# Where the first weight load of the later output projections stands in the program

## The chip, the cores and the metric

The kernel runs on one core of one Trainium2 chip. The metric is the time of one launch on the device in microseconds (us); lower is better. One execution was also taken by the profiler. A core has a matrix engine (TensorE, PE in the profile, with its weight loads as PEld), three engines for elementwise work (VectorE or DVE, ScalarE or ACT, GpSimd or POOL) and SyncE (SP), which here issues nearly all transfers between HBM and the on-chip memory (SBUF). Matmuls write to PSUM, the accumulation memory.

## The reference

One layer of a hybrid encoder is computed for 2048 new prompt frames and 32 frames of a running stream ("sample rows"), with width 1024. All is float32:

```python
h = rms_norm(x, g_norm1) * (1 + scale1) + shift1          # scales from c @ w_ada
q, k, v, z, xbc_raw, dt_raw = jnp.split(h @ w_in, SPLITS, axis=-1)
...
attn = stick_breaking(q, k, v)                            # 8 heads of 64, gated by a running product
attn = rms_norm(attn.reshape(bsz, l, SB_WIDTH), g_attn_out)
ssm, new_conv, new_ssm = ssd_mixer(z, xbc_raw, dt_raw, ...)   # conv, chunked scan, gate, rms_norm
mixed = jnp.concatenate([attn, ssm], axis=-1) @ w_out     # the output projection
x = x + gate1 * mixed
h2 = rms_norm(x, g_norm2) * (1 + scale2) + shift2
ff = (jax.nn.silu(h2 @ w_gate) * (h2 @ w_up)) @ w_down    # 2816 hidden columns
x = x + gate2 * ff
```

Returned are the new x for both inputs, and the keys, values, convolution rows and scan states.

## The kernel before, in words

**Arithmetic.** A float32 product is made of three matmuls on rounded operands: each operand is split into a high part (a copy in the reduced format, ScalarE) and a low part (the rest, by a subtraction on another engine). `mm3` (L127) issues high x high, high x low and low x high.

**Tiling and stages.** The prompt is cut into four quarters of 512 frames, g = 0 to 3; the sample rows count as g = 4. The first stage makes h, the input projection and the scan mixer, quarter by quarter. Attention follows: quarter 0 in full (`attn`), quarters 1 to 3 in a window of the last 640 keys (`attn_w`, L341), and then `far_keys` (L453), one pass over the older keys for the few rows that still need them. It walks seven chunks of 256 keys (tiles `Kf`, `Vf`), adds what it finds to the stored attention rows (`far`, `aof`), and closes. Then come the output projections (class `Wout`, L717) and the feed-forward (`ffn`, L885).

**The output projection of a quarter.** `Wout.pre` (L728) loads the scan mixer's rows (`mH`, `mL`, high and low) from the scratch tensor `mixT`, the gates (`gr`) and the rows of x (`x`, summed in place). It also holds `pf`, a list of four pieces of `w_out`, two column halves for the scan rows and two for the attention rows; I call them out A, B, C and D. `opiece` (L103) makes a piece: one load of 1024 KB into a `wr` buffer, then four times a ScalarE activation (L114) that scales by the group's norm weight and rounds into `wh`, and a VectorE operation (L115) for the low part `wl`. `Pieces.get` (L97) hands out a piece and at once asks for the next (`fill`, L93). `product` (L748) multiplies a half for four blocks of 128 frames into PSUM (tile `z`), scales by the gate into `tm` (L761) and adds to x on GpSimd (L763). `ssm` (L767) does out A and B. `rows` (L774) loads and splits the attention rows, and `run` (L838) does C and D and then the second norm, whose result goes to the scratch tensor `h2D`. `project` (L995) strings these together for one quarter.

**The feed-forward of a quarter** walks eleven pieces of 256 hidden columns. Each has a gate, an up and a down piece of weights, 1024 KB each, made by the same loads into `wr` and splits into `wh` and `wl` (ScalarE and GpSimd, L59 and L60). A piece has 96 matmuls for gate and up (tiles `pg`, `pu`) and 48 for down (`py`). Again each `get` asks for the next piece, so the up and the down weights of a piece are asked for at its start, and the next gate weights ahead of its down products.

**Shared buffers.** All weight pieces, of output projection and feed-forward alike, come from `wtiles` (L72): two `wr` buffers, three `wh` and three `wl`.

**What sets the order.** From `attn_w` of quarter 1 on, two generators are woven together by `merge` (L1700). Side A is `streamA` (L1619): the windows of quarters 1 to 3, the far keys, the projections of quarters 1 and 2, the sample rows' attention and projection, and the projection of quarter 3. Side F is `streamF`, the feed-forward of the four quarters. Each `yield` carries a planned cost in ns. A step of A with cost c adds c times a ratio to a debt, and F is stepped until the debt is paid. The ratio begins at a constant (L1642) and becomes 4.0 when quarter 1 is projected (L1631). F must not begin quarter g + 1 before A has said that it is projected (`("need", g + 1)`, L966).

The text so made is a program order. The framework (`schedule_with_timeline_sim`, L1752) then puts each instruction into its engine's queue where, in a plan of the run that it makes while building, the operands and a free buffer are there; where several are ready, the earlier one in the program goes first. So a load that needs nothing but a buffer can stand in SyncE's queue far ahead of its neighbours in the code.

The pool of a projection's own tiles (`gr`, `x1` and others) is opened for each quarter (L1626) on the memory that the attention's tiles held before.

Of the kernel before, what the change touches and what calls it, by code (L numbers as in the profile page):

```python
# [35 lines left out]
def body(tc, nc, I, O):  # L36
    V, A, G, PE = nc.vector, nc.scalar, nc.gpsimd, nc.tensor
    ctx = ExitStack()
    with ctx:
# [12 lines left out]
        def load(dst, src):  # L52
            nc.sync.dma_start(dst, src)
# [49 lines left out]
        def opiece(k0, hf, g, pool=None):  # L103

            if pool is None:
                r, h, l = wtiles()
            else:
                r = rpool[0].tile([P, WP], F32, tag="wr", name="wr", bufs=rpool[1])
                h, l = (pool.tile([P, 2048], F32R, tag=t, name=t, bufs=1) for t in ("oh", "ol"))
            v = lambda t: t[:, :2048].rearrange("p (k c) -> p k c", k=4)  # L110
            load(v(r), I["w_out"][0, k0 * P:(k0 + 4) * P, hf * 512:(hf + 1) * 512].rearrange("(k p) c -> p k c", p=P))
            r, h, l = v(r), v(h), v(l)
            for k in range(4):
                A.activation(h[:, k, :], r[:, k, :], AF.Copy, scale=g[:, k:k + 1])  # L114
                V.scalar_tensor_tensor(l[:, k, :], r[:, k, :], g[:, k:k + 1], h[:, k, :].bitcast(F32), op0=ALU.mult, op1=ALU.subtract)  # L115
            return h, l
# [81 lines left out]
        def mixed(mp):  # L198

            return [mp.tile([P, 4, 512], F32R, name=t) for t in ("mH", "mL")], mp.tile([P, 4, 4], F32, name="stat")  # L200
# [227 lines left out]
        def window_tiles(at_):  # L428
            aT = [at_.tile([P, 2, 257], F32, tag="aT", name=f"aT{i}", bufs=2) for i in range(2)]
            dd = at_.tile([P, 2, 257], mybir.dt.bfloat16, tag="d1", name="dd", bufs=1)  # L430
            for t in aT + [dd]:
                G.memset(t, 0.0)
            G.memset(dd[:, :, 256:257], 1.0)
            return aT, dd
# [3 lines left out]
        def far_consts(fc):  # L438
            io = fc.tile([P, 256], mybir.dt.bfloat16, name="io")
            G.iota(io, pattern=[[1, 256]], base=0, channel_multiplier=0, allow_small_or_imprecise_dtypes=True)  # L440
            pcol = fc.tile([P, 1], F32, name="pcol")
            G.iota(pcol, pattern=[[0, 1]], base=0, channel_multiplier=1, allow_small_or_imprecise_dtypes=True)
            hv = fc.tile([P, 9], F32, name="hv")
            G.iota(hv, pattern=[[16, 9]], base=1, channel_multiplier=0, allow_small_or_imprecise_dtypes=True)
            vt = fc.tile([P, NH, 12], F32, name="vt")
            G.iota(vt, pattern=[[16, NH], [1, 12]], base=5, channel_multiplier=0, allow_small_or_imprecise_dtypes=True)
            bk = fc.tile([P, 4], F32, name="bk")
            G.iota(bk, pattern=[[P, 4]], base=0, channel_multiplier=0, allow_small_or_imprecise_dtypes=True)
            one = fc.tile([P, P], F32R, name="one")
            G.memset(one.bitcast(F32), 1.0)  # L450
            far_c.update(io=io, pcol=pcol, hv=hv, vt=vt, bk=bk, one=one, pool=fc)
# [265 lines left out]
        class Wout:  # L717
# [10 lines left out]
            def pre(self):  # L728

                s, t0 = self.s, self.t0  # L730
                mH, mL = mHL
                for i, t in enumerate((mH, mL if s == 0 else mH[:, :, DEC:])):
                    load(t[:, :, :self.n].bitcast(F32), mixT[i, :, :, t0:t0 + self.n].rearrange("k p t -> p k t"))
                self.pf = Pieces([lambda k=k, hf=hf, g=g: opiece(k, hf, g) for k, g in ((4, gsc), (0, gac)) for hf in range(2)])
                self.pf.fill(1)
                xsrc = I["x_prompt"][0, t0:t0 + self.n] if s == 0 else I["x_sample"][0]
                self.gr, self.x1 = [], {}
                for hf in range(2):
                    t = self.tile("gr", "gr")
                    load(t.rearrange("p (m c) -> p m c", m=4), modD[16 + hf * 4:20 + hf * 4, s].unsqueeze(0).to_broadcast([P, 4, P]))  # L740
                    self.gr.append(t)
                for b, c, m in self.tb:
                    x1 = self.tile("x1", "x1", nb=len(self.tb), w=D)
                    load(x1[:m], xsrc[c:c + m])
                    for hf in range(2):
                        self.x1[hf, b] = x1[:, hf * 512:(hf + 1) * 512]
# [248 lines left out]
        def project(g, pool):  # L995
            w = Wout(g, pool, zps)
            w.pre()
            yield 3000
            yield from w.ssm()
            yield from w.run()  # L1000

# [40 lines left out]
        with ExitStack() as pa:  # L1042
# [454 lines left out]
            def run_all(g):  # L1497
                for _ in g:
                    pass
# [40 lines left out]
            def chain(*gs):  # L1540
                for g in gs:
                    yield from g
# [56 lines left out]
        with ExitStack() as pb_:  # L1599
            mp = pb_.enter_context(tc.tile_pool(name="mp", bufs=1))  # L1600
            mHL, stat = mixed(mp)
            pw0 = ExitStack()
            w0 = Wout(0, pw0.enter_context(tc.tile_pool(name="wo0", bufs=1)), dense_ps)
            w0.pre()
            merge2(a0, w0.ssm(), R1)
            pa0.close()
            fc = px_.enter_context(tc.tile_pool(name="fc", bufs=1, side="right"))
            far_consts(fc)
            L = fc.tile([P, NH, 12], F32, name="L")
            px1 = ExitStack()  # L1610
            at1 = px1.enter_context(tc.tile_pool(name="at1", bufs=1, side="right"))
            wt = window_tiles(at1)
            a1 = chain(*(attn_w(g, at1, L, wt) for g in range(1, NQ)))
            run_all(w0.run())
            pw0.close()
            fp = pb_.enter_context(tc.tile_pool(name="fp", bufs=1))
            late = {}

            def streamA():  # L1619
                yield from a1  # L1620
                yield from far_keys(at1, wt[0], L)
                px1.close()
                for g in range(1, NQ):
                    if g == 3:
                        yield from part_s()
                    with tc.tile_pool(name=f"wo{g}", bufs=1, side="right") as wo:  # L1626
                        yield from project(g, wo)
                    if g < 3:
                        yield ("done", g)
                    if g == 1:  # L1630
                        yield ("ratio", 4.0)  # L1631
                px_.close()
                late["ex"] = pb_.enter_context(tc.tile_pool(name="ex", bufs=1, side="right"))
                dpool[0] = pb_.enter_context(tc.tile_pool(name="pdF", bufs=5, space=PSUM))
                yield ("done", 3)

            def streamF():
                hT = load_h(0, fp, None)
                for g in range(NQ):
                    hT = yield from ffn(g, fp, late, hT)  # L1640

            merge(streamA(), streamF(), 1.55)  # L1642


        fx = ctx.enter_context(tc.tile_pool(name="fx", bufs=1))
# [39 lines left out]
def merge2(main, side, ratio, fin=True):  # L1685

    debt = 0.0
    for c in main:
        debt += c * ratio
        while side is not None and debt > 0:  # L1690
            try:
                debt -= max(next(side), 1)
            except StopIteration:
                side = None
    if side is not None and fin:
        for _ in side:
            pass


def merge(a, f, ratio):  # L1700
    done, debt = set(), 0.0
    a_live, f_live, need = True, True, None
    while a_live or f_live:
        blocked = a_live and need is not None and need not in done
        if not blocked:
            need = None
        if a_live and (blocked or not f_live or debt <= 0):
            try:
                c = next(a)
                if isinstance(c, tuple) and c[0] == "ratio":  # L1710
                    ratio = c[1]
                elif isinstance(c, tuple):
                    done.add(c[1])
                elif not blocked:
                    debt += c * ratio
            except StopIteration:
                a_live = False
        else:
            try:
                c = next(f)  # L1720
                if isinstance(c, tuple):
                    need = c[1]
                else:
                    debt -= c
            except StopIteration:
                f_live = False
# [29 lines left out]
```

## Time and profile before

| | |
|---|---|
| time, median of 3 runs (lowest, highest) | 2942.09 us (2938.08, 2947.04) |
| time of the profiled execution | 2940.34 us |
| its span, first to last instruction | 2938.4 us |
| mean granted clock of TensorE, as a share of full speed | 0.963 |
| busy: PE, PEld | 2729.8 us (93%), 2334.2 us (79%) |
| busy: DVE, ACT, POOL | 1563.9, 1186.0, 1532.6 us |
| moved by DMA | 466.54 MB, mean 159 GB/s |

How to read the lines. A row of a timeline has the start in us from the span's start, the length in us, the engine (SPq is SyncE's queue, where a row is the issue of a transfer), the line of the code (of a helper where a helper issues it), the operation, output tile <- input tiles, the shape, and the count of merged instructions. In square brackets stands how long the engine had been idle before and what released it. A row of a table of stretches has the stretch, its length, then busy us and count of instructions for each engine, then the granted clock of TensorE, the busy share of the DMA engines and GB/s. Matmuls overlap in such counts: a row of 0.39 us is followed by the next start after 0.23.

### The profile page before, as it was taken

Reading aid. Unit: us, or ns where it says so; the run is one execution under the profiler, and the core shown is the slowest. Engines: PE = TensorE matmul, PEld = TensorE weight load, DVE = VectorE, ACT = ScalarE, POOL = GpSimd, SP = SyncE. Lnnn points to the kernel's source line nnn. Section 1 sums busy time; section 2 is a strip of 40 time slices with the busy share of each in tenths; the row PEclk is TensorE's granted clock in tenths of the full one; section 3 lists DMA queues with packets and bytes.
Section 4 is the critical chain, followed back from the end, with each engine's and each line's share of the span. In section 5 each row is a group of like instructions: output and inputs, shape, how many; then the busy total and the mean of one; then the engine's idle time right before and its main releaser. Section 6 shows DMA issues by size and latency. Waiting matters only on the chain.

```text
span 2938.4 us, 41844 instructions
## 1 busy us (share of the span) xinstructions
PE 2729.8 (93%) x15467; PEld 2334.2 (79%) x15467; DVE 1563.9 (53%) x2575; ACT 1186.0 (40%) x2533; POOL 1532.6 (52%) x1318
## 2 busy tenths in 40 slices
PE   6998998998978689998879999999999999999998
PEld 5988997896977578876667887777787788899997
DVE  6577586766568567874344534434434422333336
ACT  6466365555535455522224334333243422322221
POOL 4767566564654635743136655544564445544445
PEclk8999998999988789999989999999999999999999
DMA  8755653463467787837745744534733722422221
GB/s 266 219 171 153 202 177 114 119 182 106 131 175 237 193 225 196 208 116 213 199 165 180 258 135 137 152 122 155 236 127 106 230 88 92 154 87 87 86 87 66
DMA packets 415619, 466.54 MB, mean 159 GB/s; under 512 B 34191, under 2 KB 330991, under 8 KB 415406
## 3 DMA queue, kind: packets, MB, share of 16 engines
q1 hardware_dynamic: 414478, 463.61, 52.7%
q8 instruction: 124, 2.03, 0.3%
q14 instruction: 89, 0.73, 0.1%
q10 hardware_dynamic: 896, 0.14, 0.0%
q0 software_dynamic: 32, 0.03, 0.0%
HBM read 372.66 MB, written 91.04 MB: 158 GB/s over the span
## 4 chain that ended last, share of the span: by engine, by line
PE 57%; DVE 6%; DMA 5%; issue 3%; POOL 2%; ACT 2%; SPq 1%; DVEq 0%; ACTq 0%; POOLq 0%
PE pg L130 5%; PE pg L131 5%; PE pg L132 5%; PE pu L130 5%; PE pu L131 5%; PE pu L132 5%; PE py L130 5%; PE py L131 4%; PE py L132 4%; PE z L130 2%; PE z L131 2%; PE z L132 1%; PE d L131 1%; PE d L130 1%; PE d L132 1%
## 5 line engine op out<-in xcount | busy, mean ns | idle before, releaser
L60 POOL TENSOR_TENSOR wl<-wr,wh 128x512 fp32r<-128x512 f32 x752 | 1010.3, 1375 | 861.7 <-ACT wh L59 778.5
L59 ACT ACTIVATE wh<-wr 128x512 fp32r<-128x512 f32 x816 | 450.3, 620 | 512.3 <-PE py L132 128.4
L130 PE MATMUL d<-wh,hH 128*128 128x256 f32 (+2 forms) x1088 | 316.0, 291 | 18.8 <-ACT hH L59 10.9
L132 PE MATMUL d<-wh,hL 128*128 128x256 f32 (+2 forms) x1088 | 311.8, 287 | 6.7 <-POOL hL L60 6.7
L130 PE MATMUL pg<-h,wh 128*128 128x512 f32 (+1 forms) x880 | 311.3, 354 | 3.7 <-POOL aT L378 2.5
L130 PE MATMUL pu<-h,wh 128*128 128x512 f32 (+1 forms) x880 | 310.5, 353 | 1.2 <-DVE sg L952 1.2
L131 PE MATMUL d<-wl,hH 128*128 128x256 f32 (+2 forms) x1088 | 311.4, 286 | 0.0
L132 PE MATMUL pg<-h,wl 128*128 128x512 f32 (+1 forms) x880 | 310.7, 353 | 0.6 <-POOL wl L60 0.6
L131 PE MATMUL pg<-h,wh 128*128 128x512 f32 (+1 forms) x880 | 310.7, 353 | 0.0
L132 PE MATMUL pu<-h,wl 128*128 128x512 f32 (+1 forms) x880 | 310.5, 353 | 0.0
L131 PE MATMUL pu<-h,wh 128*128 128x512 f32 (+1 forms) x880 | 309.9, 352 | 0.0
L130 PE MATMUL py<-wh,aH 128*128 128x512 f32 x704 | 282.5, 401 | 7.0 <-DVE ya L983 5.0
L131 PE MATMUL py<-wl,aH 128*128 128x512 f32 x704 | 277.0, 394 | 0.0
L983 DVE TENSOR_TENSOR ya<-py,ya 128x512 f32<-128x512 f32 x288 | 190.4, 684 | 148.4 <-PE py L132 146.8
L132 PE MATMUL py<-wh,aL 128*128 128x512 f32 x704 | 265.8, 394 | 2.8 <-DVE aL L60 2.8
L952 DVE TENSOR_TENSOR sg<-pg,sg 128x512 f32<-128x512 f32 (+1 forms) x110 | 64.8, 589 | 336.8 <-ACT sg L951 336.8
L130 PEld LDWEIGHTS d<-wh,hH 128*128 128x128 f32 (+1 forms) x1088 | 207.7, 191 | 23.2 <-ACT hH L59 12.5
L132 PEld LDWEIGHTS d<-wh,hL 128*128 128x128 f32 (+1 forms) x1088 | 206.9, 190 | 8.0 <-POOL hL L60 7.2
L131 PEld LDWEIGHTS d<-wl,hH 128*128 128x128 f32 (+1 forms) x1088 | 207.3, 191 | 0.7
L130 PEld LDWEIGHTS pg<-h,wh 128*128 128x128 f32 x880 | 165.6, 188 | 28.5 <-POOL aT L378 2.7
L130 PEld LDWEIGHTS pu<-h,wh 128*128 128x128 f32 x880 | 165.5, 188 | 24.2 <-DVE sg L952 1.4
L132 PEld LDWEIGHTS pg<-h,wl 128*128 128x128 f32 x880 | 165.4, 188 | 24.1 <-POOL wl L60 1.1
(434 smaller groups left out, 5686.7 us busy)
## 6 DMA issues: line engine op xcount, KB each, us to landing
wr<-in_w_in SPq DMA_DIRECT2D x48, 1024.0 KB
wr<-in_w_gate SPq DMA_DIRECT2D x44, 1024.0 KB
wr<-in_w_up SPq DMA_DIRECT2D x44, 1024.0 KB
wr<-in_w_down SPq DMA_DIRECT2D x44, 1024.0 KB
wr<-in_w_ada SPq DMA_DIRECT2D x24, 1024.0 KB
wr<-in_w_out SPq DMA_DIRECT2D x20, 1024.0 KB
h2D<-hl SPq DMA_DIRECT2D x64, 256.0 KB
Kw<-KT SPq DMA_DIRECT2D x48, 320.0 KB
```

The lines of the kernel that those rows point to most:

```text
L59: A.activation(h, src, AF.Copy)
L60: (eng or V).tensor_tensor(l, src, h.bitcast(F32), op=ALU.subtract)
L130: PE.matmul(out, lhsT=sh, rhs=mh, start=(i == 0), stop=False)
L131: PE.matmul(out, lhsT=sh, rhs=ml, start=False, stop=False)
L132: PE.matmul(out, lhsT=sl, rhs=mh, start=False, stop=(i == n - 1))
L952: V.tensor_tensor(sg[:, :n], pg[:, :n], sg[:, :n], op=ALU.mult)
L983: V.tensor_tensor(dst, ps[:r], dst, op=ALU.add)
```

## The change

```diff
@@ Wout.pre @@
                 self.pf = Pieces([lambda k=k, hf=hf, g=g: opiece(k, hf, g) for k, g in ((4, gsc), (0, gac)) for hf in range(2)])
-                self.pf.fill(1)
+                if self.g == 0:
+                    self.pf.fill(1)
                 xsrc = I["x_prompt"][0, t0:t0 + self.n] if s == 0 else I["x_sample"][0]
@@ project @@
             w.pre()
-            yield 3000
+            yield 3500
+            w.pf.fill(1)
+            yield 4500
             yield from w.ssm()
@@ body @@
-            merge(streamA(), streamF(), 1.55)
+            merge(streamA(), streamF(), 1.45)
```

Before, `pre` asks for out A between the loads of the scan rows and those of gates and x, and `project` then gives the other side 3000 times the ratio. After, only quarter 0, whose projection isn't woven by `merge`, still does so. For quarters 1 to 3 and the sample rows, `project` gives way for 3500, asks for out A (load, four activations, four VectorE operations), gives way for 4500, and goes on to the products, which ask for out B. The ratio of the weaving until quarter 1 is projected falls from 1.55 to 1.45. No arithmetic changes.

## The prediction

> **What bounds the kernel now.** I read the page first, then busy time by stretches, then the timelines of SyncE, ScalarE and TensorE around each output projection.
>
> ```profile
> span 2938.4 us, 41844 instructions
> ...
> PE 57%; DVE 6%; DMA 5%; issue 3%; POOL 2%; ACT 2%; SPq 1%; DVEq 0%; ACTq 0%; POOLq 0%
> ```
>
> The chain that ended last is mostly TensorE (PE). So an edit that moves no arithmetic can change the time only where PE stands idle or runs at its lower clock. The stretches show where that is (columns: length, then busy time and count of PE, PEld, DVE, ACT, POOL, then the granted clock and the DMA share):
>
> ```profile
> 1265.00:1430.00 165.00, 149.84 (x704) 119.93 (x703) 80.13 (x146) 41.62 (x81) 52.26 (x40) 1.00 0.63 176
> 1430.00:1502.00 72.00, 49.99 (x165) 36.11 (x166) 27.58 (x49) 4.47 (x10) 7.74 (x6) 0.74 0.67 214
> 1502.00:2340.00 838.00, 826.52 (x3653) 661.46 (x3652) 356.09 (x518) 310.66 (x622) 445.17 (x355) 1.00 0.51 163
> ```
>
> From 1502 to 2340, which holds the projections of quarters 2, the sample rows and 3, PE is idle for 838.0 - 826.5 = 11.5 us in all; there is little to win there. One matmul costs 826.52 / 3653 = 0.226 us there, the price I use below. The bad place is 1430 to 1502, the end of the far keys and the start of quarter 1's projection: 22.0 us idle and a mean clock of 0.74. Its 165 matmuls at 0.226 us are 37.3 us of work, so 72.0 - 37.3 = 34.7 us are lost there. That is the most that this edit can win at its main place.
>
> Why PE starves there is seen in what SyncE loads and when ScalarE splits it:
>
> ```profile
> 1388.51 0.54 SPq L53 DMA_DIRECT2D wr<-in_w_out  x1
> ...
> 1438.21 0.54 SPq L53 DMA_DIRECT2D wr<-in_w_out  x1
> ...
> 1451.49 0.78 SPq L53 DMA_DIRECT2D wr<-in_w_up  x1
> ...
> 1491.33 0.92 SPq L53 DMA_DIRECT2D gr<-modD  x2
> ```
> ```profile
> 1416.94 2.55 ACT L114 ACTIVATE wh<-wr,cols 128x512 fp32r<-128x512 f32 x4
> ...
> 1504.58 2.57 ACT L114 ACTIVATE wh<-wr,cols 128x512 fp32r<-128x512 f32 x4 [36.69 <-PE z L132]
> ...
> 1515.68 2.20 ACT L59 ACTIVATE wh<-wr 128x512 fp32r<-128x512 f32 x4 [0.99 <-PE z L132]
> ```
> ```profile
> 1495.27 1.41 DVE L761 SCALAR_TENSOR_TENSOR tm<-z,rsS,gr 128x512 f32<-128x512 f32 x2 [6.14 <-DMA gr<-modD]
> 1496.08 0.29 PEld L130 LDWEIGHTS z<-wh,mH 128*128 128x128 f32 x1 [8.72 <-DVE tm L761]
> 1496.08 0.79 PE L130 MATMUL z<-wh,mH 128*128 128x512 f32 x1 [8.00 <-DVE tm L761]
> ```
>
> Quarter 1's first output weights are issued at 1388.5, 103 us ahead of the gates (1491.3) that stand beside them in the code. The gates have to wait for memory that the attention still holds; the weights wait for nothing but a buffer. They are split at 1416.9 and then sit in one of the three `wh` buffers until the gates are there and the first products leave PSUM (1495.3, 1496.1). The next output weights (loaded at 1438.2) and the next up weights (1451.5) wait for the buffers of those products, until 1504.6 and 1515.7. So the feed-forward stream, which should fill PE, runs dry.
>
> **Quarter 1, step by step.** The merge's books are arithmetic on the numbers in the code. Side A spends 3 x (2500 + 8 x 2780) on the windows and 66,360 on the far keys, 140,580 in all; times 1.55 this releases 217.9 us of planned feed-forward work before quarter 1's `pre`, times 1.45 only 203.8. One feed-forward piece is 4 x 5120 for gate and up and 8 x 1296 for down, 30.85; up and down weights of piece i are asked for at 30.85 i, gate weights 10.37 before that. In whole steps the orders of the requests are:
> before: up 7, down 7, out A, out B, gate 8, out C, up 8, down 8, out D;
> after: up 6, down 6, gate 7, out A, out B, up 7, down 7, out C, gate 8, up 8, down 8, out D.
> Out A moves from planned work 221.1 to 209.5: although it is put later behind `pre`, it comes earlier against the stream, because the ratio fell. Two output pieces are still neighbours and still take two of three buffers ahead of the far keys' end.
>
> How far does the stream get before it is dry? Its matmuls, by output:
>
> ```profile
> 0.00:1265.00 1265.00, 58.12 (x212) 39.38 (x212) 5.54 (x8) 4.72 (x8) 0.93 0.63 181
> 1265.00:1430.00 165.00, 44.63 (x172) 31.33 (x172) 5.51 (x8) 4.72 (x8) 1.00 0.63 176
> 1430.00:1516.00 86.00, 6.71 (x24) 4.71 (x24) 0.69 (x1) 0.60 (x1) 0.78 0.60 192
> ```
> ```profile
> 0.00:1265.00 1265.00, 50.43 (x192) 35.73 (x192) 5.50 (x8) 0.93 0.63 181
> ```
> ```profile
> 0.00:1265.00 1265.00, 49.99 (x192) 34.34 (x192) 15.49 (x24) 4.48 (x8) 0.93 0.63 181
> ```
>
> The first fence is gate (pg, 24 a group, two groups a piece), then up (pu), then down (py, 48 a piece). Gate has 212 + 172 + 24 = 408 = 17 groups by 1516: pieces 0 to 7 and half of 8. After the change gate 8 stands behind out C, so the stream should end with down 7, 24 matmuls sooner: 24 x 0.226 = **+5.4 us** (bounds: 0 if the queues come out as now; +16.2 in the second rival below). Against it, those 24 stand between steps of the far keys, which come sooner without them, and the far keys set the time of the gates. By these rows that gives back between nothing and all 5.4; I take the middle, **-2.7**.
>
> The ratio itself I cost at nothing in the windows and far keys, because the stream runs ahead of plan there, so that attention has precedence already: by 1265 it has done 212 + 192 + 192 = 596 matmuls of 144 a piece, 4.14 pieces or 127.7 planned, against 74.22 x 1.55 = 115.0 released by the windows. If that cover is wrong, VectorE sets the windows and the smaller filling shows as PE idle: at most the 14.1 us of planned work that moves. It isn't lost then, it is done later, beside idle time, so the price is between 0 and +14.1; I take 0. The two new yields add no instruction. SyncE now passes gates and rows before out A; of the moved step every part counts: one load, four ScalarE and four VectorE instructions a piece, all there before.
>
> **Quarter 2.** With ratio 4 the delay is 8000 x 4 = 32 us of side work instead of 3000 x 4 = 12.
>
> ```profile
> 1586.57 0.38 SPq L53 DMA_DIRECT2D wr<-in_w_out  x1
> ...
> 1593.30 0.36 SPq L53 DMA_DIRECT2D mH<-mixT  x1
> ```
> ```profile
> 1600.87 0.77 PE L130 MATMUL z<-wh,mH 128*128 128x512 f32 x1 [2.38 <-DMA mH<-mixT]
> ```
> ```profile
> 1600.00:1620.00 20.00, 19.13 (x76) 15.46 (x77) 14.77 (x18) 7.08 (x16) 18.17 (x14) 0.91 0.82 262
> ```
>
> Here the output weights went out 6.7 us ahead of the rows, and PE's in-order queue stood 2.38 us for the rows, with feed-forward work behind. Then the clock fell: a mean of 0.91 over 20 us is 20 x 0.09 / 0.5 = 3.6 us at half speed, or 1.8 us lost. 20 us more of work between should hide the rows: **-4.2 us** (bounds -4.2 and 0). The Trainium skill, "TensorE: Matmul & The Clock Gate", Part 1, says that the clock is halved after at least one idle window of about 3.4 us; a gap of 2.38 us would cost only itself by that, and the term would be -2.4. The row shows a fall behind the shorter gap, and I go by the row.
>
> **Sample rows and quarter 3.** Both start later by 20 us of side work. The one place that I can price is the start of the third feed-forward quarter, where quarter 3's gates and rows now share SyncE with its loads:
>
> ```profile
> 2096.09 0.50 PE L130 MATMUL pg<-h,wh 128*128 128x512 f32 x1 [1.16 <-ACT wh L59]
> ```
>
> By the books quarter 3's `pre` moves from just ahead of that start to behind it. I take **-0.6**, half of the gap; bounds -1.2 and +1.2, since the sample rows' tail comes to lie there instead. Quarter 3 ends 51 planned us later, at 941, and the last feed-forward quarter needs it at 1008, so nothing new waits for it.
>
> **Sum.** 5.4 - 2.7 - 4.2 - 0.6 = -2.1 us. The profiled execution took 2940.34 us (span 2938.4); that gives 2938.2, call it **2938**. The three timed runs have a median of 2942.09, 1.75 above the profiled one, so the same step seen there is about 2940. About 0.3%, 8.8 us, is what a measurement here can tell from no change: I forecast no change.
>
> **Rivals.**
> *Faster: the stall at 1430 to 1502 is really broken up.* If the output weights no longer run ahead of the far keys, the stream keeps its three buffers and fills PE until the gates land. All 34.7 us is the end of it; a half, 17, is likelier because the far keys' own chain stays: 2921. For it: that is what the moved line asks for. Against it: the load at 1388.5 came far ahead since only a buffer held it, and nothing in the new order holds it back.
> *Slower: the stream is cut off a whole step earlier.* If down 7 cannot take the buffer of up 7 and must wait, like out C and up 8 now, for quarter 1's first products, down 7's 48 matmuls also fall behind the wait: (24 + 48) x 0.226 = 16.3 us without a return, less the 4.8 of the later quarters: 2940.3 + 16.3 - 4.8 = 2952. It decides from the point where down 7's split begins after the gates have landed. Against it:
>
> ```profile
> 1637.57 2.56 ACT L114 ACTIVATE wh<-wr,cols 128x512 fp32r<-128x512 f32 x4 [2.98 <-POOL wl L60]
> ```
> ```profile
> 1637.79 0.39 PE L130 MATMUL z<-wh,mH 128*128 128x512 f32 x1
> ```
>
> Quarter 2's second output piece is written at 1637.6 while the first is only beginning to be used (1637.8): it took another, freed buffer, so buffers aren't handed out in strict turn. For it: the queues are in order, and a small shift can put products ahead of down 7.
> *The late load is exposed.* From issue (1586.6) to the fence's first product (1600.9) quarter 2's weights had 14.3 us. Quarter 1 now leaves 4500 x 1.45 = 6.5 planned us between load and product; of a load and split as long as that, 7.8 us would stand bare, if only the plan covered it: 2946, which is still no change. The Trainium skill, "DMA: Bandwidth & Descriptors", Rules for kernel authors, speaks for this one: issue a DMA early, compute, and wait late. The trace agrees that early loads hide, and shows that here they do so by holding a scarce buffer for 79 us (1416.9 to 1495.3).
>
> **How the numbers follow.** Forecast 0.39 and exposed load 0.06, both no change: 0.45. Faster rival 0.32. Slower rival 0.23. The range reaches below the half-broken stall (2921) to 2912, and above 2952 to 2957; the forecast's own range is 2930 to 2946.
>
> **What would show it.** Right: out A and out B still issued far ahead of the gates near 1490; in the stall no gate 8 matmul, down 7 done before the first products; at quarter 2 no wait for the rows and clock 1.00. Wrong: feed-forward matmuls between the far keys' last steps and the first products (faster), or down 7 behind those products (slower). A stretch of the windows with more PE idle than now would break my price of zero for the ratio.

## The result and the profile after

The changed kernel takes **2979.93 us** (median of 4 runs, 2977.93 to 2984.29); the kernel before, run beside it, 2944.57 us (median of 4, 2938.08 to 2948.27). The ratio is 1.0124, with a 95% interval of 1.0102 to 1.0147: slower by some 35 us. The profiled execution of the changed kernel took 2984.29 us, with a span 44.2 us longer than before. I had forecast no change, 2938, and a range up to 2957. The time lies outside it.

From the page of the changed kernel, the span and the shares of the chain that ended last:

```profile
span 2982.6 us, 41835 instructions
...
PE 59%; DMA 7%; DVE 5%; POOL 2%; issue 2%; ACT 1%; SPq 1%; DVEq 0%; ACTq 0%; POOLq 0%
```

The three stretches of the prediction, of the changed kernel:

```profile
1265.00:1430.00 165.00, 140.52 (x629) 110.86 (x627) 63.44 (x123) 35.32 (x69) 42.49 (x35) 0.94 0.63 171
1430.00:1502.00 72.00, 43.32 (x121) 28.33 (x121) 22.78 (x43) 4.54 (x11) 5.25 (x5) 0.68 0.55 179
1502.00:2340.00 838.00, 814.02 (x3580) 653.01 (x3579) 326.70 (x491) 288.37 (x568) 430.37 (x344) 0.99 0.47 150
```

TensorE is idle for 24.5, 28.7 and 24.0 us in them, against 15.2, 22.0 and 11.5 before. So there are two places, and narrower stretches find them. First the kernel before, then the changed one:

```profile
1400.00:1520.00 120.00, 95.01 (x370) 72.19 (x369) 50.26 (x84) 20.47 (x39) 19.63 (x15) 0.84 0.64 197
2060.00:2180.00 120.00, 118.03 (x526) 94.54 (x525) 49.42 (x69) 40.04 (x77) 63.37 (x51) 1.00 0.56 189
```
```profile
1400.00:1520.00 120.00, 76.31 (x248) 52.87 (x247) 30.66 (x59) 10.35 (x24) 16.84 (x13) 0.74 0.55 165
2060.00:2180.00 120.00, 99.35 (x414) 77.28 (x413) 49.00 (x72) 37.12 (x74) 67.07 (x52) 0.91 0.61 206
```

I take as lost what is left of a stretch after its matmuls at 0.226 us each (the prediction's price). Around quarter 1 that is 120.0 - 370 x 0.226 = 36.4 us before and 120.0 - 248 x 0.226 = 64.0 after: **27.6 us more**. Around the start of the third feed-forward quarter it is 1.1 before and 26.4 after: **25.3 us more**. Together 52.9, of which the span shows 44.2. By the same count some 5 us come back from 1520 to 2060 (5.7 lost before, 0.3 after) and some 6 from 2180 to 2500 (9.2 and 3.6), where 146 matmuls of tile `z` lie now, against 71 before; the rest is the error of counting with one price. By this count the net price of the second place is nearer 20 us than 25.

**Place 1, quarter 1.** What SyncE loads for the weights in the changed kernel, and when ScalarE splits it:

```profile
1342.20 0.54 SPq L53 DMA_DIRECT2D wr<-in_w_gate  x1
1360.39 0.53 SPq L53 DMA_DIRECT2D wr<-in_w_out  x1
1378.79 0.53 SPq L53 DMA_DIRECT2D wr<-in_w_out  x1
1390.58 0.39 SPq L53 DMA_DIRECT2D wr<-in_w_up  x1
1401.58 0.38 SPq L53 DMA_DIRECT2D wr<-in_w_down  x1
1487.60 0.92 SPq L53 DMA_DIRECT2D gr<-modD  x2
```
```profile
1370.28 2.19 ACT L59 ACTIVATE wh<-wr 128x512 fp32r<-128x512 f32 x4 [3.36 <-issue]
1378.94 2.56 ACT L114 ACTIVATE wh<-wr,cols 128x512 fp32r<-128x512 f32 x4 [5.44 <-DMA Kf<-KT]
1397.71 2.56 ACT L114 ACTIVATE wh<-wr,cols 128x512 fp32r<-128x512 f32 x4 [5.37 <-PE py L132]
1499.78 2.20 ACT L59 ACTIVATE wh<-wr 128x512 fp32r<-128x512 f32 x4 [34.49 <-PE z L132]
```

The reader is to see the order gate 7, out A, out B, up 7, down 7, which is the one that the prediction worked out. Gate 7, out A and out B take all three `wh` buffers that the code has, at 1370.3, 1378.9 and 1397.7. Up 7 was loaded at 1390.6, but its split begins at 1499.8, when the products of out A (`z`) have been made. In the stretch 1400 to 1500 the feed-forward had 56 + 48 + 48 = 152 matmuls (gate, up, down) before. Now up and down have none there, and gate has this row:

```profile
1400.00:1500.00 100.00, 4.01 (x14) 2.04 (x12) 0.67 (x1) 0.60 (x1) 0.69 0.62 187
```

Those 14 are the end of gate 7's first group. Its second group, 24 matmuls whose weights were there, did not run either: in the program it comes behind the first up group. So gate 7's buffer stayed taken as well, and nothing but the first products could free one. These could not go on without the gates, loaded at 1487.6 (by the code, into memory that the far keys give back):

```profile
1491.93 0.80 PE L130 MATMUL z<-wh,mH 128*128 128x512 f32 x1 [7.21 <-DVE tm L762]
```

**Place 2, the start of the third feed-forward quarter.** TensorE first, in the changed kernel:

```profile
2100.00:2120.00 20.00, 11.90 (x55) 8.86 (x53) 11.99 (x17) 7.99 (x21) 11.41 (x9) 0.94 1.06 380
2120.00:2140.00 20.00, 13.43 (x48) 10.46 (x48) 3.81 (x4) 0.69 (x2) 9.31 (x8) 0.72 0.86 289
2140.00:2160.00 20.00, 14.34 (x51) 11.37 (x51) 8.18 (x13) 4.54 (x8) 3.82 (x3) 0.83 0.46 148
```
```profile
2126.57 0.79 PE L130 MATMUL pg<-h,wh 128*128 128x512 f32 x1 [12.96 <-DVE yt L987]
...
2145.76 0.80 PE L130 MATMUL pg<-h,wh 128*128 128x512 f32 x1 [5.66 <-DVE yt L987]
```

Each gate group waits for a PSUM tile that VectorE has yet to read (`yt`, the end of the second quarter's down products). Followed back, the first gap, the longer one, goes to GpSimd and ScalarE:

```profile
2116.51 6.22 POOL L60 TENSOR_TENSOR wl<-wr,wh 128x512 fp32r<-128x512 f32 x5 [5.31 <-ACT wh L59]
2122.70 1.25 POOL L925 TENSOR_TENSOR ya<-ya,xf 128x512 f32<-128x512 f32 x1
```
```profile
2115.77 2.22 ACT L59 ACTIVATE wh<-wr 128x512 fp32r<-128x512 f32 x4
...
2118.50 2.19 ACT L59 ACTIVATE wh<-wr 128x512 fp32r<-128x512 f32 x4 [0.31 <-DMA wr<-in_w_down]
```
```profile
2106.87 0.82 SPq L53 DMA_DIRECT2D wr<-in_w_down  x1
```

GpSimd's addition for the residual (2122.7) stands behind five weight splits of the third feed-forward quarter. They waited for ScalarE, which had the sample rows' second norm in hand as well (until 2118.2). The last of these weights also landed late: the down weights were split 11.6 us after their issue, with the DMA engines busy throughout (a share of 1.06 from 2100 to 2120). The second gap is a chain through three queues, of VectorE, GpSimd and SyncE:

```profile
2144.22 0.69 DVE L988 TENSOR_TENSOR ya<-ya,yt 128x512 f32<-128x512 f32 x1 [13.38 <-POOL ya L925]
2145.02 0.69 DVE L987 TENSOR_TENSOR yt<-py,gr 128x512 f32<-128x512 f32 x1
```
```profile
2142.93 1.26 POOL L925 TENSOR_TENSOR ya<-ya,xf 128x512 f32<-128x512 f32 x1 [13.61 <-DMA xf<-x1D]
```
```profile
2115.94 3.61 SPq L56 DMA_DIRECT2D h2D<-hl  x4
...
2126.32 0.99 SPq L53 DMA_DIRECT2D gr<-modD  x2
...
2130.23 4.78 SPq L53 DMA_DIRECT2D ao<-aoD  x2
2135.11 0.38 SPq L53 DMA_DIRECT2D xf<-x1D  x1
```

The residual's x (`xf`, one buffer) is loaded behind the gates, rows and attention rows of quarter 3 and used 7.8 us after its issue. Those loads stand in SyncE's queue behind the stores of the sample rows' tail (`h2D`, 2115.9) and a store of the residual (2125.8). When the operation that ended the first gap began (`yt`, 2125.8), they had not been issued; of quarter 3 only scan rows (2106.2) and the first output weights (2121.5) had.

The residual's end was not quick in the kernel before either. VectorE waited there for the same operation of GpSimd:

```profile
2106.81 0.69 DVE L987 TENSOR_TENSOR ya<-ya,yt 128x512 f32<-128x512 f32 x1 [2.65 <-POOL ya L924]
...
2118.01 1.75 DVE L987 TENSOR_TENSOR ya<-ya,yt 128x512 f32<-128x512 f32 x1 [2.71 <-POOL ya L924]
```

Its steps are 11.2 us apart, and yet TensorE lost 1.1 us in all. What covered them is seen in TensorE's `z` matmuls, first before, then after:

```profile
2095.00:2125.00 30.00, 17.23 (x70) 13.18 (x70) 5.16 (x7) 0.00 (x0) 1.00 0.80 283
```
```profile
2095.00:2125.00 30.00, 2.33 (x8) 1.08 (x8) 0.67 (x1) 0.59 (x1) 0.87 0.98 335
```

Before, quarter 3's gates were there and 70 of its products stood between the feed-forward groups. After, the sample rows' last 8 do.

At quarter 2 the prediction's sign did show: the scan rows go out 24 us ahead of the output weights, and the first product waits for nothing.

```profile
1610.80 0.36 SPq L53 DMA_DIRECT2D mH<-mixT  x1
...
1635.14 0.37 SPq L53 DMA_DIRECT2D wr<-in_w_out  x1
```
```profile
1658.82 0.39 PE L130 MATMUL z<-wh,mH 128*128 128x512 f32 x1
```

### The profile page after: what moved, and what is told of

It reads as the page before. It is cut to its first block, busy times and chain, and to the rows that moved or that the text cites. A ratio compares the mean times of both kernels' runs of the same rounds, so it can differ in the third digit from the quotient of the medians.

```text
span 2982.6 us, 41835 instructions
## 1 busy us (share of the span) xinstructions
PE 2741.7 (92%) x15467; PEld 2339.1 (78%) x15467; DVE 1543.3 (52%) x2575; ACT 1185.7 (40%) x2533; POOL 1533.2 (51%) x1318
## 4 chain that ended last, share of the span: by engine, by line
PE 59%; DMA 7%; DVE 5%; POOL 2%; issue 2%; ACT 1%; SPq 1%; DVEq 0%; ACTq 0%; POOLq 0%
PE pg L130 5%; PE pg L131 5%; PE pg L132 5%; PE pu L130 5%; PE pu L132 5%; PE pu L131 5%; PE py L130 5%; PE py L131 4%; PE py L132 4%; DMA Vf<-VS 2%; PE z L130 2%; PE z L131 1%; PE z L132 1%; PE d L131 1%; PE d L130 1%
## 5 line engine op out<-in xcount | busy, mean ns | idle before, releaser
L958 DVE TENSOR_TENSOR sg<-pu,sg 128x512 f32<-128x512 f32 (+1 forms) x110 | 65.0, 591 | 253.9 <-PE pu L132 252.9
L764 POOL TENSOR_TENSOR x<-x,tm 128x512 f32<-128x512 f32 (+1 forms) x68 | 96.2, 1419 | 179.7 <-DMA x<-in_x_prompt 118.7
```

The source lines that it names most:

```text
L764: G.tensor_tensor(x1[:m], x1[:m], tm[:m], op=ALU.add)
L958: V.tensor_tensor(sg[:, :n], pu[:, :n], sg[:, :n], op=ALU.mult)
```

## Experiments

My theory after the result: place 1 comes from the ratio alone (it puts out A and out B ahead of up 7), and place 2 from where the sample rows' tail and quarter 3's loads fall against the start of the third feed-forward quarter. The rivals: the later request itself makes place 1, and the new pauses themselves make place 2. The table has the losses as counted above; the expectations count idle time and half of the time at half clock instead, which gives up to 3 us less or more. The kernel before was run again beside each set, with medians of 2940.28 to 2944.57, and each ratio goes by its own set. "Books" is where the sample rows end in the planned feed-forward work, in planned us; the third feed-forward quarter begins at 679.

| kernel | median us | ratio to before (95%) | lost 1400-1520 | lost 2060-2180 | books |
|---|---|---|---|---|---|
| before | 2944.57 | | 36.4 | 1.1 | 658 |
| changed | 2979.93 | 1.0124 (1.0102 to 1.0147) | 64.0 | 26.4 | 684 |
| changed, ratio back | 2945.24 | 1.0015 (0.9996 to 1.0035) | 36.8 | 13.6 | 704 |
| before, ratio 1.45 only | 2962.07 | 1.0074 (1.0052 to 1.0095) | 63.0 | 0.4 | 637 |
| changed, gate groups first | 2970.26 | 1.0104 (1.0064 to 1.0144) | 42.0 | 18.1 | |
| changed, pauses of 1 and 2 only | 2960.01 | 1.0061 (1.0042 to 1.0080) | 63.5 | 4.5 | 663 |
| later requests in 1 and 2 | 2926.18 | 0.9949 (0.9932 to 0.9965) | 30.1 | 2.0 | 653 |
| before, quarter 3 later | 2952.76 | 1.0039 (1.0029 to 1.0049) | 40.2 | 16.7 | 658 |
| before, sample rows and 3 later | 2963.33 | 1.0060 (1.0039 to 1.0080) | 35.9 | 26.0 | 684 |
| later request in 1 only | 2939.33 | 0.9990 (0.9978 to 1.0001) | 29.1 | 3.4 | 653 |
| later request in 2 only | 2942.12 | 1.0001 (0.9989 to 1.0012) | 37.7 | none | 658 |
| changed, second ratio 3.7 | 2969.32 | 1.0092 (1.0078 to 1.0107) | 61.5 | 9.5 | 658 |
| changed, quarter 3 behind | 2983.68 | 1.0133 (1.0108 to 1.0158) | 64.2 | 26.4 | 684 |

**The two halves of the edit.** The changed kernel with the old ratio, and the kernel before with the new one:

```diff
-            merge(streamA(), streamF(), 1.45)
+            merge(streamA(), streamF(), 1.55)
```

> The changed kernel with the ratio of the weaving back at 1.55; both new yields and the later load stay. Theory: in quarter 1 the ratio alone did the harm, because it moved the requests for output pieces A and B ahead of up 7; back at 1.55 they stand behind up 7 and down 7 again, so the stall from 1400 to 1520 loses about 37 us as before (after: 62) and feed-forward runs into piece 8 before it. The second loss, 24 us at the start of the third feed-forward quarter, belongs to the yields and stays in part (10 to 24), since the sample rows' projection still ends behind that start. Time 2950 to 2966. Rival: the moved load itself starves quarter 1; then the stall stays near 62 and the time near 2980.

> The kernel before with the ratio at 1.45 and nothing else. Theory: requests come in the order out A, gate 7, out B, up 7, so feed-forward stops after the first gate group of piece 7, and quarter 1 loses about 62 us as after the change, 25 more than before; nothing is lost at the start of the third feed-forward quarter, because quarter 3's first loads lie well ahead of it. Time 2965 to 2975. Rival (the moved load did it): within 5 us of before, 2940 to 2949.

The stretch 1400 to 1520, with the old ratio in the changed kernel, then with the new ratio in the old one:

```profile
1400.00:1520.00 120.00, 94.09 (x368) 70.72 (x367) 49.20 (x83) 20.48 (x39) 19.00 (x15) 0.86 0.65 198
```
```profile
1400.00:1520.00 120.00, 75.73 (x252) 53.24 (x251) 31.91 (x60) 10.80 (x24) 16.44 (x13) 0.73 0.55 166
```

So place 1 is the ratio's, all of it: 368 matmuls without it, 252 with it alone. The later request has no part in it. The first kernel's time came 5 us below the band that I gave; its loss at place 2 lay inside what I expected, and some 6 of the 12.5 us more that it loses there come back from 2180 to 2500 (9.2 lost before, 3.1 here). The second came 3 us below its band.

**Why the stream stops so early.** In the changed kernel both gate groups of a piece are written ahead of the up groups (for the first three feed-forward quarters), so that gate 7's buffer can be given back:

```diff
...
+                        if last:
+                            sg = front(j, n0, n)
+                            yield 24 * n / 2.4
+                        else:
+                            for jj in range(2) if j == 0 else ():
+                                sgs[jj] = front(jj, n0, n)
+                                yield 24 * n / 2.4
+                            sg = sgs.pop(j)
```

> The changed kernel with both gate groups of a feed-forward piece written ahead of both up groups. Theory: the second gate group did not run in the stall since its PSUM tile is given out in program order behind the first up group's tile, whose weights had no buffer; written ahead of it, it runs, gives gate 7's buffer to up 7, and down 7 follows. Feed-forward then reaches the end of piece 7 before the stall and quarter 1 loses 40 to 48 us instead of 62; the 24 us later stay. Time 2960 to 2970. Rival: the second gate group waits for something else (no buffer, or the far keys come first); then nothing changes, 2980 within 5.

```profile
1406.07 2.19 ACT L59 ACTIVATE wh<-wr 128x512 fp32r<-128x512 f32 x4 [1.95 <-issue]
```
```profile
1400.00:1520.00 120.00, 90.85 (x345) 68.11 (x344) 42.14 (x75) 19.90 (x39) 30.15 (x24) 0.83 0.61 189
```

The requests still come as gate 7, out A, out B, up 7, down 7, but up 7 is split at 1406.1, not at 1499.8, and the feed-forward reaches the end of piece 7 before the wait. With 345 matmuls, 97 of the 122 that the change had pushed out of the stretch are back. That shows that gate 7's buffer, held for a group that stood behind the up group, closed the ring. Whether the PSUM order or the buffers of `sg` kept that group back was not told apart. The time gained less (2970.26), since this order loses elsewhere: TensorE is idle for 9.2 us from 1660 to 2060 and for 6.6 from 2180 to 2500, against 1.9 and 1.9 in the changed kernel. It is no remedy.

**Whose pauses make place 2.** The new request order only in quarters 1 and 2, with the new ratio:

```diff
+            yield 3500 if g in (1, 2) else 3000
+            w.pf.fill(1)
+            if g in (1, 2):
+                yield 4500
```

> The changed kernel with the new yields and the later load for quarters 1 and 2 alone; sample rows and quarter 3 as before. Theory: the loss of 24 us at the start of the third feed-forward quarter comes from the sample rows' tail and quarter 3's loads being moved into it; planned 20 us earlier each, the sample rows end before it and the loss falls below 8. Quarter 1 keeps its 62. Time 2958 to 2968. Rival: that loss follows from the lag that quarter 1 leaves; then it stays above 15 and the time near 2980.

Place 2 shrinks to 4.5 us. That alone doesn't say whether the pauses of the sample rows and of quarter 3 do it by themselves or by their place, so the kernel before was given a delay there, and nothing else:

```diff
         def project(g, pool):
+            if g >= 3:
+                yield 6500 if g == NQ else 9000
```

The first of the two kernels delays only quarter 3 (6500), the second both:

> The kernel before with a pause of 6500 (at ratio 4) ahead of quarter 3's projection alone: the sample rows' projection keeps its place ahead of the third feed-forward quarter, quarter 3's weights, gates and rows are asked for 5 us behind its start, as in the changed kernel. Theory with quarter 3's loads as the cause of the loss there: 10 to 20 us lost from 2060 to 2180, 2950 to 2960. Theory with the sample rows' tail as the cause: under 4 us lost and 2940 within 5.

> The kernel before with a pause of 6500 ahead of the sample rows' projection and 9000 ahead of quarter 3's: the sample rows' second norm ends 5 us behind the start of the third feed-forward quarter, as in the changed kernel, and quarter 3's loads come 36 planned us later still. Theory with the sample rows' tail as the cause: 10 to 20 us lost from 2060 to 2180 and 2950 to 2960. Theory with quarter 3's loads as the cause: under 4 us lost there and 2940 within 5.

```profile
2060.00:2180.00 120.00, 108.19 (x457) 85.85 (x456) 39.33 (x52) 34.03 (x66) 60.76 (x48) 0.96 0.54 181
```
```profile
2060.00:2180.00 120.00, 100.11 (x416) 78.36 (x416) 39.28 (x57) 37.66 (x75) 63.78 (x50) 0.91 0.57 195
```

Quarter 3 alone, moved behind that start, loses 16.7 us; its products are then gone from 2095 to 2125 (none; 69 of them come from 2125 to 2160). With the sample rows' tail in it as well, 26.0 are lost, as in the changed kernel, to 0.4. I had set the two causes against each other, and neither fits alone: this second kernel is above both of its bands, in loss and in time. Its gaps are 11.72 and 6.55 us, with the same two chains as in the changed kernel. No output weight is asked for in another order here. So place 2 is a matter of place alone, though not a simple one: with the old ratio the sample rows end later still (704), there is no `z` matmul from 2095 to 2125 either, and 13.6 us are lost. The same from the other side is the changed kernel with its second ratio at 3.7, by which the sample rows end at 658 again:

> The changed kernel with one number altered: the second ratio 3.7 in place of 4.0, so that the sample rows end by the books at 658 in place of 684, ahead of the start of the third feed-forward quarter (679) as before. If the loss at that start comes from where the sample rows' tail and quarter 3's loads lie, 2060 to 2180 loses under 10 us in place of 25.9 and the time falls to 2955 to 2965; quarter 1's loss stays at 60 to 65. If the two yields of the sample rows and quarter 3 themselves do it, whatever their place, it stays at 2975 to 2982.

```profile
2060.00:2180.00 120.00, 114.76 (x489) 90.83 (x488) 48.53 (x66) 38.16 (x75) 73.87 (x57) 0.99 0.60 200
```

The loss falls from 26.4 to 9.5, with quarter 1's left as it was. The median came 4 us above the band: this kernel's runs spread from 2961.77 to 2974.63, and the profiled one is at the low end.

A last attempt was to part quarter 3's loads from the sample rows' tail inside the changed kernel, by 8000 of delay ahead of quarter 3:

> The changed kernel with one addition: 8,000 units of side work ahead of quarter 3's projection, so that its gates, rows and x are asked for by the books at 720, behind the start of the third feed-forward quarter (679), while the sample rows' tail stays where the change has put it (684). If quarter 3's loads, waiting on SyncE ahead of the residual's loads, are what stops the start (theory), 2060 to 2180 loses 5 to 14 us in place of 25.9, the gap of 5.66 us before the second gate group goes, and the time is 2960 to 2970. If the sample rows' tail alone stops it (rival), it still loses 22 or more and the time stays at 2976 to 2984. Quarter 1 loses 60 to 65 either way.

```profile
2126.46 0.99 SPq L53 DMA_DIRECT2D gr<-modD  x2
```

It told nothing apart. The gates went out at 2126.46, as in the changed kernel (2126.32), though the program asks for them 36 planned us later. In both they stand directly behind the same store of the residual; that they wait there for the memory of the sample rows' tail is likely, and not shown. What the gaps of the changed kernel do say is this: the first, 12.96 us and 1.9 more at half clock, had been settled before quarter 3's gates, x and attention rows were issued, so of the two only the second, 5.66 and 2.7 us, can be theirs. How far quarter 3's products would have covered either gap stays open.

**Is the idea of the edit worth anything?** If out A is really kept back until the stream has up and down weights, it should help. For that, quarter 1 must give way for longer, and quarter 2 as the change has it:

```diff
+            if g == 1:
+                yield 17500
+                w.pf.fill(1)
+                yield ("ratio", 1.3)
+                yield 3000
+            elif g == 2:
+                yield 3500
+                w.pf.fill(1)
+                yield 4500
...
-                        yield ("ratio", 4.0)
+                        yield ("ratio", 3.6)
```

> The kernel before with quarter 1's first output weights asked for truly late: a pause of 17500 at ratio 1.55 ahead of the request, then ratio 1.3 for the rest of quarter 1, the new yields for quarter 2, and a second ratio of 3.6 so that the sample rows and quarter 3 keep their places. The requests then come as gate 8, out A, up 8, down 8, out B, out C, gate 9, and the feed-forward can run to the end of piece 8 before it needs a buffer that quarter 1 holds. Theory: the loss from 1400 to 1520 falls from 37 us to 12 to 22, the wait of 2.4 us for quarter 2's rows goes, and the time is 2915 to 2930. Rival: the far keys' own chain and the in-order queue make the stall whatever the feed-forward has left; then the loss stays above 32 and the time within 5 us of before.

```profile
1400.00:1520.00 120.00, 95.67 (x398) 73.69 (x397) 49.88 (x89) 22.99 (x44) 19.83 (x16) 0.89 0.68 206
```

It beats both kernels: 0.9949, and the stretch has 398 matmuls against 370. But the loss there is 30.1, where I expected 12 to 22, so of the four runs' 15.3 us only 6.3 are seen in it. The profiled span (2920.0) is 18.4 us shorter than before; 7.7 of these are there already at 1302 us, ahead of the edit (a load of up weights issued at 1301.54, before at 1309.21), so the profiled run was a good one. Then each half of it by itself, with the second ratio set to 3.8 so that the sample rows end where they should:

> Only quarter 1's first output weights are asked for later (17,500 units of side work behind gates, rows and x, ratio 1.3 while it waits); quarter 2, the sample rows and quarter 3 keep the order of before, with a second ratio of 3.8 so that the sample rows end by the books at 653, ahead of the third feed-forward quarter (679). If the order of the requests in quarter 1 is what made the gain of the run with both late requests (30.2 us lost from 1400 to 1520 against 37.0), this one keeps most of it: 2926 to 2934, and from 2060 to 2180 it loses under 8 us. If the gain came from quarter 2's part, it stands at 2938 to 2944.

> Only quarter 2's first output weights come behind the rows (3,500 units, the load, 4,500 units), with a second ratio of 3.8 so that the sample rows end by the books at 658, as before. My term for quarter 2 says -4.2 us, bounds -4.2 and 0: 2937 against 2941, no wait for the rows at quarter 2's first product, and no other window changed by more than 3 us. If the late load is exposed or the stream is cut instead, 2944 or more.

Neither half is a gain that can be told from nothing. Quarter 1's half keeps its own stretch (402 matmuls) but loses it again from 1520 to 1660, where the second feed-forward quarter begins and its gate group stands for its rows:

```profile
1641.72 0.71 PE L131 MATMUL pg<-h,wh 128*128 128x512 f32 x1 [2.61 <-DMA h<-h2D]
```

TensorE is idle there for 7.1 us, against 2.7 before. Quarter 2's half is without its wait for the rows (first product at 1633.03, none before it), and yet the time is 1.0001. Why the two together give 15 us and apart nothing is not settled; quarter 2's products, put later, may be what fills that start, but no run tried it.

## Why the prediction was wrong

- **The order of the requests** was right as far as the trace shows it, from gate 7 to down 7, and so was the remark that two output pieces still run ahead of the far keys' end.
- **Quarter 1, "the stream should end with down 7, 24 matmuls sooner", +5.4**: this is the step that failed. It counted pieces in the queue and took for granted that up 7 and down 7 find buffers. There are three, and out A, out B and half-used gate 7 had them. The stream ended 144 matmuls sooner, not 24: gate 7's second group, up 7, down 7 and gate 8's first group, 24 + 48 + 48 + 24 (gate has 360 matmuls by 1500, before 408; up and down 336 each, before 384). The stretch 1400 to 1520 has 122 fewer in all, and 122 x 0.226 = 27.6 us.
- **"Gives back between nothing and all 5.4; -2.7"**: the far keys did come sooner, the gates' load at 1487.6 against 1491.3, 3.7 us. The loss of 64.0 has that in it.
- **The ratio "I cost at nothing"**: the price was looked for in the windows, and in the windows it is about right (from 1265 to 1400 TensorE is idle 9.5 us after, 12.2 before). But the ratio had already been used, two paragraphs above, to move out A ahead of up 7; by the run with the ratio alone that move is worth 22 us (1.0074). I priced one effect of the number and not the other, though I had written both down.
- **Quarter 2, -4.2**: the wait went as foretold, and in the changed kernel the stretch 1520 to 2060 is idle for 3.0 us against 6.9. Alone it bought nothing (1.0001, 0.9989 to 1.0012).
- **Sample rows and quarter 3, -0.6 with bounds of 1.2**: the second failure, and the larger surprise. I saw that quarter 3's `pre` moves behind the start of the third feed-forward quarter and that "the sample rows' tail comes to lie there instead", and bounded that by the one wait visible there, 1.16 us. That wait was small while 70 products of quarter 3 stood beside a residual whose steps are up to 11 us apart. With the products gone, and the sample rows' tail and quarter 3's loads in their place, the price is 25.3; which of these weighs how much is not settled. A visible wait bounds what can be won at a place, not what can be lost there.
- **The rivals.** The slower one has the mechanism: a feed-forward piece that finds no buffer and waits for quarter 1's first products. It named down 7, with 72 matmuls and 2952; it was up 7 already, with 144. Its counter-evidence, buffers not handed out in strict turn at quarter 2, was beside the point: with three buffers held there is no other to hand out. It had no part for place 2. The faster rival did not come about: nothing held the output weights back. Even in the kernel with later requests the stretch loses 30.1 against 36.4, far from the half that the rival names. The late load was not exposed. The Trainium skill's rule beside it ("DMA: Bandwidth & Descriptors", Rules for kernel authors: issue a DMA early, wait late) does not settle it here: out A came early, was split at 1378.9, and kept a buffer from up 7 until 1499.8.

## What to carry to other kernels

When two streams share a ring of buffers, an early request is not free: write down who holds each buffer at the moment of the longest wait, and check that the stream which must fill that wait can still give one back. Price a changed ratio or pause by everything that it moves in the books, out to the last place before the next fixed point, and at each such place ask what covers the slow work there now, since the small wait that a profile shows is what is left after the cover. When a reordering loses, take its parts one by one on the chip: here one number alone cost 22 of the 35 us, and an arrangement that really asks late, with the ratios behind it changed too, gains 0.5%, for reasons not yet told apart.

## What the runs showed of the hardware

At place 2 TensorE's clock came back only some time after a gap. Behind the gap of 12.96 us it stood at half for 4.4 us, behind that of 5.66 us for 5.8 us (changed kernel), so the shorter gap had the longer half-clock time behind it:

```profile
2126.57:2131.00 4.43, 4.43 (x11) 3.46 (x11) 1.38 (x2) 0.00 (x0) 2.74 (x3) 0.50 0.70 207
2131.40:2139.00 7.60, 7.60 (x34) 6.08 (x33) 0.00 (x0) 0.00 (x0) 0.00 (x0) 1.00 1.04 389
2145.76:2151.60 5.84, 5.84 (x14) 4.64 (x15) 2.08 (x3) 1.08 (x2) 1.31 (x2) 0.50 0.61 201
2152.00:2159.00 7.00, 7.00 (x31) 5.61 (x30) 4.63 (x7) 3.04 (x5) 0.85 (x1) 1.00 0.24 80
```

By the rows, 11 matmuls in 4.43 us are 2.49 us of work at 0.226, and 14 in 5.84 are 3.16: these two gaps cost 1.9 and 2.7 us beyond their own length. The Trainium skill, "TensorE: Matmul & The Clock Gate", Part 1, has the clock whole again after at least one busy window of about 3.4 us. Here 4.4 and 5.8 us are both longer than one such window, which the page's "at least" allows.
